# The gated sum of an encoder layer taken by halves of the tokens, its loads in order of use, and the w_out split moved from GpSimd to VectorE

## The chip, the core and the metric

One core of a Trainium2 chip runs the whole kernel. The metric is the device time of one execution in microseconds (us). The engines are TensorE (PE), VectorE (DVE), ScalarE (ACT), GpSimd (POOL) and SyncE (SP). Each works through its own list of instructions in order, and semaphores tie the lists together. Matmul results land in PSUM (8 banks of 128 x 512 fp32), everything else on the chip lies in SBUF, and DMAs bring data from HBM.

## What is computed

Two layers of an encoder over 1024 tokens and 1024 channels. The part that matters here, of one layer, is:

```
ya = mla_branch(...)                    # ends in  o @ w_oa,   o: 1024 x 512
merged = gates[:, :, 0] * ya + gates[:, :, 1] * yb + gates[:, :, 2] * yc
x = x + g1 * (merged @ w_out[l])
h2 = rmsnorm(x, norm2_g[l]) * (1.0 + sc2) + sh2
x = x + g2 * ec_moe(h2, w_router[l], w_gate[l], w_up[l], w_down[l])
```

`gates[0]` and the finished sum of the two other products are computed earlier and wait in HBM (`gate0d`, `partd`, 8 blocks of 128 channels x 1024 tokens each). `w_out` times `g1` also waits there (`woutd`). Products keep fp32 accuracy: an operand is split into `hi` (rounded by ACT) and `lo = x - hi` (a subtraction), and three matmuls (hi hi, hi lo, lo hi) replace one.

## The kernel before

The program is written in Python; a scheduler fixes the order of every engine's list when the kernel is built, and tiles of a pool are reused in rotation, so that a load waits until the last reader of its buffer is done.

After attention (lines 904 to 952) comes the **gated sum**: for each of the 8 blocks d of channels, `merge_mm` (L942) multiplies `w_oa` with `o` (`ohi`, `olo`: 4 blocks of 128 x 1024 tokens) into a PSUM tile of two banks, 24 matmuls of 512 columns, written by `mm3` (L319, the matmul at L325). `merge_gate` (L966) then takes each half of the tokens: loads `gate0d` (L970) and `partd` (L972) into two tiles `gh` (six buffers in all), multiplies (L973, one operand in PSUM), adds (L974, both in SBUF), and splits the result into the tiles `gm` by `split` (L114: a cast on ACT, a subtraction on VectorE, both at L115). The first two blocks stand around the last attention product `av(7, 3)`, whose result goes through `otmp` (L881) and `op` (L884) into `ohi` and `olo` of the second half of the tokens.

Meanwhile `w_out` is loaded in four quarters of 256 columns (`wout_load`, L980, 1 MB each) and split by `wout_split` (cast on ACT at L990, subtraction on POOL at L991).

Then comes the **output product**, one tile t of 128 tokens after the other (loop at L1227). `out_mm` (L1135, matmul at L1142) runs 96 matmuls of 256 columns for a tile; `residual` (L1145) adds the row of x, which ACT's list loads (L1229); `x_trans` (L1164) transposes the row on PE, `router` (L1177) multiplies it with the router, `soft` (L1185) makes a softmax. The tile t = 0 takes the quarters one by one and needs all 8 blocks d of the gated sum; from t = 1 on, the transposes, the router and, from t = 2 on, rounds of a top-k search on VectorE (`fills`, L1056) are woven in. The loads of the first expert weights (`prefetch`, L1033) start here too. SP issues all loads but the x rows.

The weights of `w_oa` lie in three pairs: `wo0` (columns 0 to 255), `wo1` (256 to 511) and `wo2` (512 to 1023, L996); their raw copies and those of `w_out` share two buffers named `raw`, and the pair of `wo2` takes buffers that `av(7, 3)` reads last.

Of the kernel before, what the change touches and what calls it, by code (L numbers as in the profile page):

```python
# [19 lines left out]
D = 1024  # L20
# [34 lines left out]
def encoder(ctx, tc, x, c, positions, w_mod, b_mod, norm1_g, w_in, b_gate, q_norm_g, w_uq, kv_norm_g,  # L55
# [271 lines left out]
    for l in range(DEPTH):  # L327
# [450 lines left out]
        with pool("att", side="right") as ap:  # L778
# [110 lines left out]

            LA = 2  # L890
# [13 lines left out]
            for n, (h, t) in enumerate(units):  # L904
# [6 lines left out]
                if n >= 1 and units[n - 1][1] % 2 == 1:  # L911
# [4 lines left out]
                    av(hh, g, *phl.pop((hh, g)), po[hh])  # L916
                if h % 2 == 0 and t == 2:
# [24 lines left out]
            def merge_mm(p, wo, c0, k0, k1):  # L942
                cs_ = slice(c0, c0 + 128)
                for k in range(k0, k1):
                    mm3(p, wo[0][:, k, cs_], wo[1][:, k, cs_], ohi[:, k], olo[:, k], k == 0, k == 3)
# [18 lines left out]
        wos = {}  # L964
# [12 lines left out]
        def wout_load(q):  # L977

            raw = W.tile([128, 8, 256], F32, name="raw", tag="raw")
            SP.dma_start(raw, woutd[l][:, :, 256 * q:256 * q + 256].rearrange("k p f -> p k f"))  # L980
            if q in (1, 2):
                hi, lo = (ring_tile([128, 8, 256]) for _ in range(2))
            else:
                hi = W.tile([128, 8, 256], F32R, name="whi", tag="whi")
                lo = W.tile([128, 8, 256], F32R, name="wlo", tag="wlo")
            wos[q] = (raw, hi, lo)

        def wout_split(q):
            raw, hi, lo = wos[q]
            ACT.copy(hi, raw)  # L990
            POOL.tensor_sub(lo, raw, f(hi))  # L991
            wos[q] = (hi, lo)
# [569 lines left out]
```

## Time and profile before

| | us |
|---|---|
| median of 3 runs | 3388.4 (3385.19 to 3395.47) |
| the profiled execution | 3388.24 |
| its span from the first to the last instruction | 3386.5 |
| PE busy | 3201.4 (95%) |
| VectorE busy | 2442.3 (72%) |
| ACT busy | 1857.7 (55%) |
| POOL busy | 384.2 (11%) |

The shares are means over stages. The stage between attention and the experts stands twice in the span, from about 900 and from about 2569 us, and the rows further down read the second. A row of a timeline gives start, length, engine, line, operation, output and inputs with their sizes, and in brackets how long the engine had been idle and what ended that.

### The profile page before, as it was taken

What the parts mean: (1) busy time and instruction counts of PE and PEld (TensorE: products, weight loads), DVE (VectorE), ACT (ScalarE), POOL (GpSimd) and SP (SyncE); (2) the same over time, 40 slices, a digit from 0 to 9 for tenths busy, and PEclk for the clock granted to TensorE, in tenths of its full rate; (3) what the DMA queues carried; (4) which work ended last, traced back from release to release, by engine and by line L of the source; (5) the groups of instructions that cost most, each with busy time, mean ns of one, the idle gap of its engine ahead of it and who ended that gap; (6) DMA issues with size and microseconds to landing.
All of it is one profiled execution on the core that took longest, in us unless ns stands there. A gap on an engine that the chain in (4) does not pass through costs nothing.

```text
span 3386.5 us, 43057 instructions
## 1 busy us (share of the span) xinstructions
PE 3201.4 (95%) x16593; PEld 2672.0 (79%) x16593; DVE 2442.3 (72%) x3730; ACT 1857.7 (55%) x2535; POOL 384.2 (11%) x364
## 2 busy tenths in 40 slices
PE   6999999999978899999989999999998969999996
PEld 5888887788877688888778888887887968888875
DVE  5556525599848899999864355338997489999997
ACT  5111213588634788887631121317885448888876
POOL 2001001000034001001020000010001330001010
PEclk8999999999988899999999999999999979999998
DMA  6346334000445899999622444340015559999994
GB/s 222 118 151 203 125 114 162 33 17 13 138 177 217 301 390 381 388 391 373 254 60 81 132 157 149 103 156 17 20 38 171 199 193 358 387 389 380 389 378 176
DMA packets 283374, 686.00 MB, mean 203 GB/s; under 512 B 24935, under 2 KB 139841, under 8 KB 283169
## 3 DMA queue, kind: packets, MB, share of 16 engines
q1 hardware_dynamic: 247008, 563.13, 44.8%
q0 software_dynamic: 33856, 111.74, 10.4%
q10 hardware_dynamic: 2304, 8.39, 0.7%
q8 instruction: 130, 2.13, 0.3%
q14 instruction: 76, 0.61, 0.1%
HBM read 607.63 MB, written 75.55 MB: 202 GB/s over the span
## 4 chain that ended last, share of the span: by engine, by line
PE 77%; DVE 12%; ACT 4%; DMA 3%; issue 2%; POOL 1%; SPq 0%; POOLq 0%; DVEq 0%; ACTq 0%
PE ps L325 62%; PE pa L1142 4%; DVE wlo L115 3%; PE pa L325 2%; DVE mx L846 2%; PE pa L864 2%; PE ps L1351 1%; PE pa L872 1%; PE pa L874 1%; DMA gh<-gate 1%; ACT pexp L851 1%; ACT whi L115 1%; DVE af L1065 1%; PE pa L1183 1%; DVE top L1063 1%
## 5 line engine op out<-in xcount | busy, mean ns | idle before, releaser
L115 DVE TENSOR_TENSOR wlo<-rg,whi 128x1024 fp32r<-128x1024 f32 x768 | 899.5, 1219 | 99.2 <-ACT whi L115 95.7
L115 ACT CAST whi<-rg 128x1024 fp32r<-128x1024 f32 x768 | 763.8, 1048 | 181.0 <-PE ps L325 181.0
L325 PE MATMUL ps<-whi,T 128*128 128x512 f32 x3072 | 841.8, 393 | 4.0 <-ACT T L115 2.2
L325 PEld LDWEIGHTS ps<-whi,T 128*128 128x128 f32 x3072 | 574.8, 189 | 126.4 <-ACT T L115 3.1
L325 PE MATMUL ps<-wlo,T 128*128 128x512 f32 x1536 | 489.1, 400 | 5.0 <-DVE wlo L115 3.0
L325 PE MATMUL ps<-hhi,whi 128*128 128x512 f32 x1376 | 427.4, 392 | 0.0
L325 PE MATMUL ps<-hlo,whi 128*128 128x512 f32 x1376 | 423.9, 389 | 0.0
L325 PE MATMUL ps<-hhi,wlo 128*128 128x512 f32 x1376 | 423.8, 389 | 0.0
L325 PEld LDWEIGHTS ps<-wlo,T 128*128 128x128 f32 x1536 | 281.3, 189 | 74.3 <-DVE wlo L115 19.0
L115 ACT CAST whi<-raw 128x2048 fp32r<-128x2048 f32 (+2 forms) x59 | 101.1, 1713 | 417.1 <-PE ps L325 360.8
L325 PEld LDWEIGHTS ps<-hhi,whi 128*128 128x128 f32 x1376 | 256.9, 188 | 58.9 <-issue 4.2
L325 PEld LDWEIGHTS ps<-hlo,whi 128*128 128x128 f32 x1376 | 258.3, 188 | 54.1
L325 PEld LDWEIGHTS ps<-hhi,wlo 128*128 128x128 f32 x1376 | 258.3, 188 | 54.0
L1142 PE MATMUL pa<-rg 128*128 128x256 f32 x768 | 191.4, 304 | 28.1 <-DVE rg L115 13.4
L115 DVE TENSOR_TENSOR wlo<-raw,whi 128x2048 fp32r<-128x2048 f32 (+2 forms) x59 | 120.9, 2050 | 98.5 <-ACT whi L115 98.5
L1142 PEld LDWEIGHTS pa<-rg 128*128 128x128 f32 x768 | 148.9, 206 | 31.3 <-DVE rg L115 14.5
L325 PE MATMUL ps<-khi,raw 128*128 128x512 f32 x512 | 166.5, 406 | 7.2 <-ACT pexp L851 5.7
L115 DVE TENSOR_TENSOR wlo<-pa,whi 128x512 fp32r<-128x512 f32 x256 | 169.3, 680 | 1.3 <-ACT whi L115 1.1
L1444 POOL DMA_INDIRECT xres<-y,idx x30 | 72.5, 2416 | 779.4 <-DVE y L1443 779.4
L851 ACT ACTIVATE pexp<-ps,nm 128x1024 f32<-128x1024 f32 x128 | 143.1, 1118 | 30.4 <-DVE nm L848 27.9
L846 DVE TENSOR_REDUCE mx<-ps 128x1 f32<-128x1024 f32 x128 | 155.0, 1212 | 5.4 <-PE ps L325 4.5
L115 ACT CAST whi<-pa 128x512 fp32r<-128x512 f32 x256 | 139.6, 588 | 7.6 <-PE pa L864 6.5
(409 smaller groups left out, 4899.6 us busy)
## 6 DMA issues: line engine op xcount, KB each, us to landing
rg<-in_w_gate_dram SPq DMA_DIRECT2D x128, 1024.0 KB, 8.9
rg<-in_w_up_dram SPq DMA_DIRECT2D x128, 1024.0 KB, 6.9
rg<-in_w_down_dram SPq DMA_DIRECT2D x128, 1024.0 KB, 7.8
raw<-in_w_mod_dram SPq DMA_DIRECT2D x48, 1024.0 KB, 5.4
raw<-in_w_in_dram SPq DMA_DIRECT2D x43, 1024.0 KB, 5.2
part<-pr POOLq DMA_DIRECT2D x32, 512.0 KB, 4.9
pr<-part POOLq DMA_DIRECT2D x16, 512.0 KB, 4.3
sq<-in_w_out_dram POOLq DMA_DIRECT2D x16, 512.0 KB, 4.4
```

The costliest lines, as they stand in the source:

```text
L115: return ACT.copy(hi, src), DVE.tensor_sub(lo, src, f(hi))
L325: PE.matmul(dst[:, s], a, b[:, s], start=start and i == 0, stop=stop and i == 2)
L846: DVE.reduce_max(mx, p, axis=AX.X)
L851: ACT.activation(e, p, AF.Exp, bias=nm, scale=SCALE, accum_out=sm)
L864: PE.transpose(p[:, 128 * k:128 * k + 128], e[:, o:o + 128], ident)
L872: PE.matmul(po[:, o:o + 256], vt[:, k, h, :], phi[:, k, :], start=(k == 0), stop=False, skip_group_check=True)
L874: PE.matmul(po[0:64, o:o + 256], vt[:, k, h, 0:64], plo[:, k, :], start=False, stop=(k == 7), skip_group_check=True)
L1063: DVE.max(v[:, 15 - r, :], a)
L1065: DVE.match_replace(a, v[:, 15 - r, :], a, -1.0)
L1142: PE.matmul(p[q // 2][:, 256 * (q % 2):256 * (q % 2) + 256], a, wos[q][b][:, k, :], skip_group_check=True, start=(k == 0 and i == 0 and q ...
L1183: PE.matmul(pls[t][:, :E], hT[:, 128 * k:128 * k + 128], wra[:, kk, :], start=(kk == 0), stop=(kk == 7))
L1444: POOL.indirect_dma_start(out=xres[l], in_=y, in_offset=None, compute_op=OP.add, out_offset=bass.IndirectOffsetOnAxis(ap=idx[e][:, 0:1], a ...
```

## The change

The gated sum runs by halves of the tokens: 16 units (hf, d) of 12 matmuls and one PSUM bank each, all d of the first half (tokens 0 to 511), then d = 2 to 7, 0, 1 of the second. The loads of a unit are issued three units ahead (`gate_load`), in the order in which the units use them. The load of `wo2` and the first three pairs of gate loads are written inside the attention loop. `w_out` is handled in four blocks (half of the columns, half of the rows) of 512 columns, loaded after units 3, 6, 9 and 11 and split after units 5, 8, 11 and 14, with the subtraction on VectorE (`split`). The output product uses 48 matmuls of 512 columns for a tile, and tile 0 takes the same form as the others. The rows of x for tiles 0 and 1 are loaded first, and the first four expert loads wait for the second of them.

```diff
+            merges = [(0, d) for d in range(8)] + [(1, (d + 2) % 8) for d in range(8)]
+            to_load, gates = list(merges), {}
+            def gate_load():
+                if to_load:
+                    hf, d = to_load.pop(0)
+                    s_ = slice(512 * hf, 512 * hf + 512)
+                    gates[hf, d] = [op_.tile([128, 512], F32, name="gh", tag="gg", bufs=6) for _ in range(2)]
+                    for t_, src in zip(gates[hf, d], (gate0d, partd)):
+                        SP.dma_start(t_, src[l][d][:, s_])
...
+                if h == H - 1 and t == 6:
+                    gate_load()
+                    wo1 = load_split(cols(w_oa[l], 256, 256), 4, 256)
+                    gate_load()
+                    wo2_raw = W.tile([128, 4, 512], F32, name="raw", tag="raw")
+                    SP.dma_start(wo2_raw, cols(w_oa[l], 512, 512))
+                    gate_load()
...
-            pm = [ps2(), ps2()]
-            merge_mm(pm[0], wo0, 0, 0, 3)
+            pm = [ps2() for _ in range(2)][1]
+            for d in range(2):
+                merge_mm(pm[:, 512 * d:512 * d + 512], wo0, 128 * d, 0)
             av(7, 3, *phl.pop((7, 3)), po[7])
-            merge_mm(pm[1], wo0, 128, 0, 3)
-            for d in range(2):
-                merge_mm(pm[d], wo0, 128 * d, 3, 4)
-        psum_open(3, 2)
+        psum_open(0, 8)
...
-        def merge_gate(p, d):
-            for hf in range(2):
-                s_ = slice(512 * hf, 512 * hf + 512)
-                g0 = op_.tile([128, 512], F32, name="gh", tag="gg", bufs=6)
-                SP.dma_start(g0, gate0d[l][d][:, s_])
-                pr = op_.tile([128, 512], F32, name="gh", tag="gg", bufs=6)
-                SP.dma_start(pr, partd[l][d][:, s_])
-                DVE.tensor_mul(g0, p[:, s_], g0)
-                DVE.tensor_add(g0, g0, pr)
-                split(gm[hf][0][d // 4][:, d % 4], gm[hf][1][d // 4][:, d % 4], g0)
+        def merge_gate(p, hf, d):
+            g0, pr = gates.pop((hf, d))
+            DVE.tensor_mul(g0, p, g0)
+            DVE.tensor_add(g0, g0, pr)
+            split(gm[hf][0][d // 4][:, d % 4], gm[hf][1][d // 4][:, d % 4], g0)
+            gate_load()
...
-            ACT.copy(hi, raw)
-            POOL.tensor_sub(lo, raw, f(hi))
...
+            split(hi, lo, raws.pop((c_, kh)))
...
+        wo2 = [W.tile([128, 4, 512], F32R, name=n_, tag=n_) for n_ in ("whi", "wlo")]
+        split(wo2[0], wo2[1], wo2_raw)
         for d in range(2):
-            merge_gate(pm[d], d)
-        for d in range(2, 8):
...
+            merge_gate(pm[:, 512 * d:512 * d + 512], 0, d)
+        for i, (hf, d) in enumerate(merges):
+            if i < 2:
+                continue
+            p = ps1()
+            wo, c0 = ((wo0, 0), (wo1, 256), (wo2, 512), (wo2, 512))[d // 2]
+            merge_mm(p, wo, 128 * d - c0, hf)
+            merge_gate(p, hf, d)
+            if i in (3, 6, 9, 11):
+                wout_load(*divmod((3, 6, 9, 11).index(i), 2))
+            if i in (5, 8, 11, 14):
+                wout_split(*divmod((5, 8, 11, 14).index(i), 2))
...
-                        for q in qs:
-                            PE.matmul(p[q // 2][:, 256 * (q % 2):256 * (q % 2) + 256], a, wos[q][b][:, k, :], skip_group_check=True,
-                                      start=(k == 0 and i == 0 and q == (fst[0] if q < 2 else 2)), stop=(k == 7 and i == 2))
+                    for i, (a, b) in enumerate(((a_hi, b_hi), (a_hi, b_lo), (a_lo, b_hi))):
+                        PE.matmul(p[c_], a, b, start=(k == 0 and i == 0), stop=(k == 7 and i == 2))
...
-            prefetch(2 + N_WM)
+            for t in range(2):
+                first = row_load_x(t)
+            prefetch(2 + N_WM, first)
```

How the order moves on SP, first layer, from the load of `wo2` (1 MB, `raw<-in_w_oa_dram`) on; `gh<-gate` and `gh<-part` are the two loads of a unit, `raw<-woutd` is a block of `w_out`. Before:

```order
L313 DMA raw_7395<-in_w_oa_dram 128x4x512
L970 DMA gh_7421<-gate00_85 128x512
L972 DMA gh_7423<-part0_83 128x512
L980 DMA raw_7401<-woutd0_88 128x8x256
L980 DMA raw_7480<-woutd0_88 128x8x256
L970 DMA gh_7429<-gate00_85 128x512
L972 DMA gh_7431<-part0_83 128x512
```

And now, to the fifth unit (number 4):

```order
L935 DMA raw_7302<-in_w_oa_dram 128x4x512
L901 DMA gh_7304<-gate00_85 128x512
L901 DMA gh_7305<-part0_83 128x512
L994 DMA raw_7447<-woutd0_88 128x4x512
L901 DMA gh_7393<-gate00_85 128x512
L901 DMA gh_7394<-part0_83 128x512
L994 DMA raw_7516<-woutd0_88 128x4x512
L901 DMA gh_7401<-gate00_85 128x512
L901 DMA gh_7402<-part0_83 128x512
```

The two first blocks of `w_out` no longer stand side by side, and the loads of one unit stand between them; the scheduler has put the block written after unit 6 ahead of unit 4's loads.

On VectorE, the middle of the gated sum. Before, one block d with both halves of the tokens (`gh<-ps` multiplies, `gh<-gh` adds, `rg<-gh` is the subtraction of the split):

```order
L973 TENSOR_TENSOR gh_7550<-ps_7525,gh_7550 128x512
L973 TENSOR_TENSOR gh_7558<-ps_7525,gh_7558 128x512
L974 TENSOR_TENSOR gh_7550<-gh_7550,gh_7552 128x512
L974 TENSOR_TENSOR gh_7558<-gh_7558,gh_7560 128x512
L115 TENSOR_TENSOR rg_7384<-gh_7550,rg_7382 128x512
L115 TENSOR_TENSOR rg_7388<-gh_7558,rg_7386 128x512
```

And now, the end of unit 8 and unit 9:

```order
L115 TENSOR_TENSOR rg_7383<-gh_7487,rg_7381 128x512
L986 TENSOR_TENSOR gh_7512<-pa_7564,gh_7512 128x512
L987 TENSOR_TENSOR gh_7512<-gh_7512,gh_7513 128x512
L115 TENSOR_TENSOR wlo_7632<-raw_7585,whi_7631 128x2048
L115 TENSOR_TENSOR rg_7561<-raw_7516,rg_7560 128x2048
L115 TENSOR_TENSOR rg_7383<-gh_7512,rg_7381 128x512
```

Two of the four subtractions of `w_out` (128x2048), which stood on POOL, stand side by side between the add and the subtraction of unit 9.

On PE, tile 0 of the output product at the first transpose. Before (`pa<-whi` and `pa<-wlo` are matmuls of the last quarter, `L1183` is the router):

```order
L1142 MATMUL pa_7731<-whi_7699,rg_7382 128x256
L1142 MATMUL pa_7731<-wlo_7700,rg_7382 128x256
L1142 MATMUL pa_7731<-whi_7699,rg_7384 128x256
L1169 MATMUL pa_7836<-ident_96,xo_7728 128x128 x4
L1183 MATMUL pa_7843<-wra_134,hT_7841 128x16 x4
```

And now:

```order
L1149 MATMUL pa_7769<-wlo_7632,rg_7377 128x512
L1149 MATMUL pa_7769<-whi_7631,rg_7379 128x512
L1175 MATMUL pa_7779<-ident_96,xo_7728 128x128 x4
L1149 MATMUL pa_7769<-whi_7631,rg_7377 128x512
L1149 MATMUL pa_7769<-wlo_7632,rg_7377 128x512
```

The transpose of tile 0's first half now stands after 33 of the tile's 48 matmuls instead of after all of its 96. VectorE's list still has the first residual of tile 0 behind the last subtraction of the gated sum, and ACT's list still has the loads of the x rows behind the last cast of it.

## Rows read from the trace of the kernel before

**Rows 1.** Chain of waits: start us, length us, what; last attention copy, first router, both layers

```profile
900.68 0.59 ACT otmp L881
...
975.01 1.06 PE pa L1183 x8
...
2569.24 0.59 ACT otmp L881
...
2643.60 1.06 PE pa L1183 x8
```

**Rows 2.** Stretches of the second layer: busy us and instructions by engine, clock, DMA

```profile
2569.30:2612.00 42.70, 40.63 (x171) 32.79 (x169) 28.70 (x34) 14.52 (x16) 13.45 (x3) 0.96 0.60 205
2612.00:2641.20 29.20, 15.29 (x96) 14.33 (x97) 15.75 (x18) 6.22 (x9) 6.75 (x4) 0.71 0.66 238
```

**Rows 3.** Timeline of PE, end of the gated sum and tile 0

```profile
2611.19 0.61 PE L325 MATMUL ps<-ohi,wlo 128*128 128x512 f32 x2
2613.13 2.39 PE L1142 MATMUL pa<-rg 128*128 128x256 f32 x18 [1.33 <-DVE gh L973]
...
2630.17 5.48 PE L1142 MATMUL pa<-rg 128*128 128x256 f32 x25 [4.07 <-DVE rg L115]
```

**Rows 4.** Timeline of VectorE, the whole gated sum of the second layer

```profile
2573.03 2.29 DVE L115 TENSOR_TENSOR wlo<-raw,whi 128x2048 fp32r<-128x2048 f32 x1 [1.11 <-ACT whi L115]
2575.24 1.28 DVE L973 TENSOR_TENSOR gh<-ps,gh 128x512 f32<-128x512 f32 x2
...
2582.48 0.69 DVE L973 TENSOR_TENSOR gh<-ps,gh 128x512 f32<-128x512 f32 x1 [2.36 <-DMA gh<-gate]
...
2595.68 0.69 DVE L973 TENSOR_TENSOR gh<-ps,gh 128x512 f32<-128x512 f32 x1 [4.48 <-DMA gh<-gate]
...
2597.66 5.53 DVE L115 TENSOR_TENSOR rg<-gh,rg 128x512 fp32r<-128x512 f32 x2
...
2612.30 0.69 DVE L973 TENSOR_TENSOR gh<-ps,gh 128x512 f32<-128x512 f32 x1 [4.73 <-DMA gh<-gate]
...
2619.54 0.69 DVE L973 TENSOR_TENSOR gh<-ps,gh 128x512 f32<-128x512 f32 x1 [2.65 <-DMA gh<-gate]
...
2623.93 5.59 DVE L974 TENSOR_TENSOR gh<-gh 128x512 f32<-128x512 f32 x2
2629.44 1.45 DVE L115 TENSOR_TENSOR rg<-gh,rg 128x512 fp32r<-128x512 f32 x2
```

**Rows 5.** Timeline of POOL, three of its four w_out subtractions

```profile
2597.08 4.96 POOL L991 TENSOR_TENSOR wlo<-raw,whi 128x2048 fp32r<-128x2048 f32 x1 [12.19 <-ACT whi L990]
2608.12 4.59 POOL L991 TENSOR_TENSOR rg<-raw,rg 128x2048 fp32r<-128x2048 f32 x1 [6.08 <-ACT rg L990]
2623.96 5.00 POOL L991 TENSOR_TENSOR wlo<-raw,whi 128x2048 fp32r<-128x2048 f32 x1 [11.25 <-ACT whi L990]
```

**Rows 6.** Chain of waits, runs of PE: 512 columns, 256 columns slow, 256 columns

```profile
2517.23 4.13 PE pa L325 x18
...
2644.66 3.28 PE pa L1142 x18
...
2648.80 2.97 PE pa L1142 x24
```

**Rows 7.** Tile gh over the whole span: issue to landing of its loads

```profile
DMA to landing us min/median/max: 2.6/3.8/7.8
```

**Rows 8.** Tile gh, loads issued from 2588 to 2591 us, behind a w_out load

```profile
DMA to landing us min/median/max: 6.9/6.9/7.0
```

**Rows 9.** Tile gh, loads issued from 2596 to 2599 us, with nothing ahead

```profile
DMA to landing us min/median/max: 2.8/2.8/2.8
```

**Rows 10.** Timeline of ACT: the loads of the x rows

```profile
2629.55 1.56 ACTq L1229 DMA_DIRECT2D xo<-xres  x3
```

**Rows 11.** Tile xo, the load issued from 2656 to 2658 us

```profile
DMA to landing us min/median/max: 3.2/3.2/3.2
```

**Rows 12.** Stretch of the sixth tile of the second layer, columns as in rows 2

```profile
2713.50:2728.00 14.50, 13.83 (x118) 13.66 (x117) 14.08 (x69) 6.84 (x13) 5.45 (x5) 1.00 0.29 110
```

More of the change, by code (lines that the diff above doesn't have):

```diff
@@ L1010, in encoder, with wout_load @@
-        wout_split(0)
-        wout_load(3)
-        wout_split(3)
+        wos, raws = {}, {}
+        def merge_gate(p, hf, d):
[4 more added lines that the diff above has]
+            gate_load()
+        def wout_load(c_, kh):
+            raws[c_, kh] = W.tile([128, 4, 512], F32, name="raw", tag="raw")
+            SP.dma_start(raws[c_, kh], woutd[l][4 * kh:4 * kh + 4, :, 512 * c_:512 * c_ + 512].rearrange("k p f -> p k f"))
@@ new lines, in wout_split @@
+        def wout_split(c_, kh):
+            if c_ == 0:
+                hi, lo = (ring_tile([128, 4, 512]) for _ in range(2))
+            else:
+                hi = W.tile([128, 4, 512], F32R, name="whi", tag="whi")
+                lo = W.tile([128, 4, 512], F32R, name="wlo", tag="wlo")
+            split(hi, lo, raws.pop((c_, kh)))
+            wos[c_, kh] = (hi, lo)
+        wo2 = [W.tile([128, 4, 512], F32R, name=n_, tag=n_) for n_ in ("whi", "wlo")]
+        split(wo2[0], wo2[1], wo2_raw)
@@ L1223, in aff_trans, with row_load_x @@
                     fill.extend([lambda r=r: top_round(i, r) for r in range(16)] + [lambda: merged(i)])
-            fst = [1]
-            prefetch(2 + N_WM)
+            def row_load_x(t):
+                xos[t] = op_.tile([128, D], F32, name="xo", tag="xo", bufs=3)
+                return ACT.dma_start(xos[t], x_in[128 * t:128 * t + 128, :])
+            for t in range(2):
+                first = row_load_x(t)
+            prefetch(2 + N_WM, first)
             for t in range(8):
-                xos[t] = op_.tile([128, D], F32, name="xo", tag="xo", bufs=3)
-                ACT.dma_start(xos[t], x_in[128 * t:128 * t + 128, :])
+                if t > 1:
+                    row_load_x(t)
                 p = [ps1()]
-                if t == 0:
-                    p.append(ps1())
-                    out_mm(t, p, (1,), 0, 8)
-                    out_mm(t, p, (2,), 0, 8)
-                    out_mm(t, p, (0,), 0, 8)
-                    residual(t, p, 0)
-                    out_mm(t, p, (3,), 0, 8)
-                    fst[0] = 0
-                    residual(t, p, 1)
-                    x_trans(t, 0)
-                    router(t, 0)
-                    continue
-                out_mm(t, p, (0, 1), 0, 3)
-                x_trans(t - 1, 1)
-                scale(t - 1)
-                out_mm(t, p, (0, 1), 3, 7)
-                router(t - 1, 1)
-                soft(t - 1)
-                h2_rows(t - 1)
-                if t == 7:
-                    with behind(softs[-1]):
-                        ACT.activation(small.tile([128, 1], F32, name="ms"), epsc, AF.Sqrt)
-                out_mm(t, p, (0, 1), 7, 8)
+                out_mm(t, p, 0, 0, 3)
+                if t > 0:
+                    x_trans(t - 1, 1)
+                    scale(t - 1)
+                out_mm(t, p, 0, 3, 7)
+                if t > 0:
+                    router(t - 1, 1)
+                    soft(t - 1)
+                    h2_rows(t - 1)
+                    if t == 7:
+                        with behind(softs[-1]):
+                            ACT.activation(small.tile([128, 1], F32, name="ms"), epsc, AF.Sqrt)
+                out_mm(t, p, 0, 7, 8)
                 residual(t, p, 0)
```

48 lines of the change are left out of this document (12 added, 36 removed).

## The prediction

> **What bounds the kernel now.** I read the chain of waits first. In each layer some 74.3 us pass from the last copy of attention to the router of tile 0: 975.01 - 900.68 in the first, 2643.60 - 2569.24 in the second [rows 1]. The two layers agree, so I work in the second and count twice. Next the stretches: in the gated sum PE is busy 40.6 of 42.7 us, but in the 29.2 us after it only 15.3, at a mean granted clock of 0.71 [rows 2]. So the gain to be had lies after the gated sum, not in it. PE's timeline tells why: the last matmul of the sum is done at 2611.8, tile 0 starts, and it can run through only from 2630.17, released by VectorE [rows 3]. Tile 0 needs all 8 blocks d, and the last subtraction of the last block ends at 2629.44 + 1.45 = 2630.9 [rows 4].
>
> So VectorE's list is the chain, and its 55.7 us from 2575.24 to 2630.9 [rows 4] can be taken apart. Work: 48 operations at 0.6 (two in a row take 1.28, of which 0.08 is the tail of the second [rows 4]) are 28.8. Waits for loads: 2.36 + 4.48 + 4.73 + 2.65 = 14.2 [rows 4]. Operations stretched beside POOL: 5.53 and 5.59 where two take 1.28 [rows 4], against POOL's 4.96 and 5.00 [rows 5], 4.3 each, 8.6 together. That makes 51.6; the rest is waits for casts and smaller stretches.
>
> What stretches is visible too: the multiply at 2612.30, with one operand in PSUM, took its 0.69 while POOL ran from 2608.12 to 2612.71 [rows 4, 5]; the adds and subtractions, with both in SBUF, did not. The Trainium skill (SBUF — State Buffer, "Who interferes with whom") says just this: a VectorE instruction with two SBUF inputs and a GpSimd instruction that reads SBUF exclude each other for the whole instruction. By that rule four POOL subtractions would put up to some 19 us on VectorE in a layer; the trace shows about 9, since VectorE was often waiting anyway, and the measurement decides.
>
> **The change part by part.** *Matmuls of the gated sum.* 192 as before, now each with weights of its own; 18 such took 4.13 [rows 6], 0.229 each. Two units (24 matmuls) stand ahead of the last attention product, in the order some three more than before, so it ends about 0.7 later, at 2569.7; the other 168 take 38.5: PE is done at 2608.2, against 2611.8. It needs no wait on the way: a unit reuses the bank of eight units before, and the second half's `ohi` is due only after eight units.
>
> *VectorE.* The cast of `wo2` waits for the last attention product and now stands before `otmp`: 2569.8 to 2571.7; its subtraction (2.29 [rows 4]) ends at 2574.0; then `op`, cast, `olo` and the two waiting subtractions of units 0 and 1, to 2577.3. From there:
> 14 units x 3 x 0.6 = 25.2;
> four `w_out` subtractions of 2.29 less the overlap, 2.25 each: 9.0, new on VectorE, with the 8.6 beside POOL gone in return;
> five places in the order where a subtraction stands right behind its own cast, 0.7 each: 3.5;
> waits for loads, which is the open term.
> A load lands in 2.8 us with nothing ahead [rows 9], in 6.9 behind a 1 MB block [rows 8], 2.6 to 7.8 over all [rows 7]. A unit's loads go out when the unit three before has given its buffers back. Following the order with 2.8, and 5.5 (between the two rows, nearer to the upper, since fewer small loads stand behind the blocks now) for a load right behind a block: unit 4's add waits about 1.3, unit 8's 2.3, unit 12's 2, unit 13 1.2, unit 15 1.7. Unit 8 as the example: unit 5 gives its buffers back at 2591.1, the gate goes out at 2591.2, the `w_out` block at 2591.8, the second load at 2592.4, which lands at 2597.9; VectorE stands at the add from 2595.6. Together about 9. Bounds: 0, and the 14.2 of today.
> The sum is 2577.3 + 25.2 + 9.0 + 3.5 + 9 = 2624.0; with the ends of the waits 2615 to 2629. Today it is 2630.9.
>
> *Tile 0.* Its first half of the columns needs only the first half's `gm` and `w_out` blocks split by about 2606, so PE goes on at 2608.2 and after 33 matmuls, at 2615.8, reaches the transpose. This needs the first residual, which stands behind the last subtraction on VectorE, and the row of x, whose load stands on ACT behind the last cast. Today that load is issued at 2629.55, at the end of the sum [rows 10], where 512 KB with nothing in the way land in 3.2 [rows 11]; the expert loads that stood beside it now wait for it. So: last cast 2624, row landed 2627.5, residual 0.7, transpose at 2628. PE idles 12 us. After such idling the clock is the lower of the two levels (1.2 GHz, not 2.4): 25 matmuls in 5.48, 0.22 each, against 24 in 2.97, 0.12 [rows 3, 6]. Hence transpose 0.7, 12 matmuls of 512 at 0.41 = 4.9, router 1.0, three matmuls 0.7: tile 1 starts at 2635.3. Today it starts at 2644.5, and its first 18 matmuls take 3.28 where 2.2 would do, with the transposes after them still slow [rows 6], about 1.6 lost, which I take as gone. Gain 9.2 + 1.6 = 10.8.
>
> *Tiles 1 to 7.* 96 x 0.12 = 11.5 becomes 48 x 0.229 = 11.0: 0.5 each while PE leads. In the sixth tile VectorE is busy 14.08 of 14.5 [rows 12], so there it is hidden. I count four tiles, 2.0 (bounds 0 and 3.7). The search after the last tile stays.
>
> *Loads of the gates and experts.* The experts' first four loads now start after the x rows, near 2628; first use is near 2787, so nothing waits. The rows `sh2` and `a2` on POOL come earlier, at 2608, 1 MB in the way of the last units' loads; that is in unit 13's 1.2.
>
> A layer gains 10.8 + 2.0 = 12.8, two layers 25.6. The profiled execution took 3388.24 (span 3386.5), the median is 3388.4: **3363**.
>
> **The rivals.** *VectorE keeps up*: no load waits, the sum ends at 2615, the transpose comes near 2619, a short idle; tile 1 at 2625. 19.5 + 1.6 + 3 = 24 a layer, 3340. For it: the loads are issued three units ahead in order of use. Against: the six buffers are the same, and the order puts two `w_out` blocks directly ahead of loads, one even between a unit's two.
>
> *The loads set the pace*: with 6.9 for each, three units take 6.9 + 2.8 (multiply, add, cast, subtract), 3.2 a unit, 45 for 14, and half of the 9.0 beside: the sum ends at 2627 to 2630. Tile 1 at 2641: 3.5 + 1.6 + 2 = 7 a layer, 3374. For it: 14.2 us of load waits today. Against: 2.8 where nothing stands ahead.
>
> *VectorE too loaded (slower).* The Trainium skill (Perfetto Trace Analysis, "Optimizing Scalar/DVE Operations") advises taking work off a saturated VectorE, and adds that between it and GpSimd this might not help, as they share a port; the change does the opposite of the advice. VectorE is busy 28.7 of 42.7 us in the sum, the stretched time included, so it is not saturated today [rows 2]. As a mechanism of this kernel: the four subtractions stand in VectorE's list, they free the `raw` buffers for which the next block's load waits, and SP's list holds the gate loads behind that. If every load lands only in the 7.8 of the slowest, three units take 10.6, 14 units 49.5, and with the 9.0 not hidden the sum ends at 2636, tile 1 starts at 2647. It turns into a loss when the sum ends later than 2637, that is with 22 us of load waits instead of 9; at 2640 the layer loses 3, the kernel 6: 3394.
>
> *The change does not do what it says*: if PE had to wait in the gated sum for its banks or for `wo2`, it would come out unchanged; the order gives `wo2` 3 us and the banks eight units of room. I give that no case of its own beyond "same".
>
> **How the numbers follow.** Chances: forecast (3350 to 3372) 0.57, VectorE keeps up (3328 to 3350) 0.18, loads set the pace (3372 to 3380) 0.17, slower than that up to no change (to 3398) 0.05, a loss 0.03. The forecast's own width is its load waits, 4 us a layer to either side, and 2 for the clock. A range of 3338 to 3377 leaves out about 0.07 below and 0.12 above. A measurement of this kernel can tell about 0.3%, 10 us, from no change: below 3378 is faster, 0.89; within 10, 0.08; above, 0.03.
>
> **What would show it right or wrong.** In the changed profile: the last matmul of the gated sum 39 us after the last attention copy; no stretched add or subtraction on VectorE; the last subtraction of the gated sum 55 us after that copy (46 for the first rival, 60 for the second); PE idle about 12 us before tile 0's transpose, with the x row as the releaser, and slow matmuls after it; tile 1 about 66 us after the copy, where it was 75; tiles of 13.8 us instead of 14.3. It is wrong above all if the load waits are not near 9 a layer, or if the x row or the residual is reached without waiting for the last unit.

## The result, and the profile after

| | before | after |
|---|---|---|
| median, us | 3386.8 | 3344.7 |
| ratio, 95% interval | | 0.9873, [0.9859, 0.9886] |
| span of the profiled execution, us | 3386.5 | 3342.1 |
| VectorE busy | 2442.3 (72%) | 2434.5 (73%) |
| POOL busy | 384.2 (11%) | 346.5 (10%) |

The change gains 42 us, where 25.6 were forecast. 3344.7 lies in the forecast range, beyond the forecast's own case and in that of the first rival. Neither case happened as it was described, though: a gain was underrated, the load waits that were forecast did not come, and a wait that the forecast had ruled out did. One of the four executions of the changed kernel took 9556 us, and one of the four with the split of `wo2` put back (further down) 5999 us; the ratios leave both out, and the medians of the other three are 3344.1 and 3347.0 us.

The zero point of all stages is the end of the last attention product, 2569.2 before (the copy L881 follows at once [rows 1]) and 2549.15 after (the cast of `wo2` follows at once). Chain of waits of the changed kernel, second layer (start, length, what); the last three rows are the first and the last router of the tiles and the first matmul of the experts:

```profile
2549.17 1.91 ACT whi L115
...
2554.16 40.52 PE pa L325 x167
...
2597.80 5.60 DMA xo<-xres
...
2607.66 0.80 PE pa L1189 x8
...
2713.03 1.90 PE pa L1189 x8
...
2745.07 1.04 PE ps L325 x2
```

And two rows of the chain of before that the forecast had not read, the same last router and first expert matmul:

```profile
2755.22 1.90 PE pa L1183 x8
2787.20 12.98 PE ps L325 x53
```

| us after the zero point | before | forecast | after |
|---|---|---|---|
| last matmul of the gated sum done | 42.6 | 39.0 | 45.5 |
| last subtraction of it done | 61.7 | 54.8 | 50.0 |
| tile 0's first transpose | | 58.8 | 55.1 |
| tile 1 starts | 75.4 | 66.1 | 60.0 |
| last tile's last router | 186.0 | 173.1 | 163.9 |
| first matmul of the experts | 218.0 | 205.2 | 195.9 |

(The forecast's last two rows: 66.1 and before's 110.6 for the tiles, less its 1.6 and 2.0; and 218.0 less its 12.8.) A layer gains 22.1 us here, 15.4 up to tile 1 and 6.7 in the tiles; two layers make the 44 of the spans. In the first layer the same stretch goes from 218.3 to 195.3.

Stretches of the second layer, columns as in rows 2:

```profile
2554.20:2560.00 5.80, 5.80 (x15) 4.60 (x16) 2.46 (x4) 1.60 (x3) 0.00 (x0) 0.57 0.74 271
2560.00:2594.70 34.70, 34.70 (x154) 28.72 (x153) 30.76 (x40) 13.97 (x15) 0.00 (x0) 1.00 0.69 220
2594.70:2604.20 9.50, 7.67 (x34) 6.01 (x32) 5.04 (x9) 1.85 (x3) 1.06 (x2) 1.00 0.74 285
```

PE's idle time has moved. Before, it stood behind the sum [rows 2]; now 4.9 us of it stand ahead of the sum's third unit (number 2), and the low clock behind it (0.57 of full speed) lets 15 matmuls take the time of 25. PE's timeline names both waits that are left:

```profile
2554.16 0.80 PE L325 MATMUL pa<-ohi,whi 128*128 128x512 f32 x1 [4.91 <-DVE op L884]
...
2604.24 0.66 PE L1175 MATMUL pa<-ident,xo 128*128 128x128 f32 x4 [1.87 <-DVE xo L1154]
```

VectorE's timeline, answering to rows 4:

```profile
2551.10 2.29 DVE L115 TENSOR_TENSOR wlo<-raw,whi 128x2048 fp32r<-128x2048 f32 x1 [1.19 <-ACT whi L115]
2553.43 0.68 DVE L884 TENSOR_TENSOR op<-pa,otmp 64x512 f32<-64x512 f32 x1
...
2559.53 0.69 DVE L986 TENSOR_TENSOR gh<-pa,gh 128x512 f32<-128x512 f32 x1 [2.65 <-PE pa L325]
...
2575.89 0.69 DVE L986 TENSOR_TENSOR gh<-pa,gh 128x512 f32<-128x512 f32 x1 [0.64 <-PE pa L325]
...
2597.84 1.30 DVE L115 TENSOR_TENSOR rg<-gh,rg 128x512 fp32r<-128x512 f32 x2
2603.49 0.69 DVE L1154 TENSOR_TENSOR xo<-xo,pa 128x512 f32<-128x512 f32 x1 [4.36 <-DMA xo<-xres]
```

No operation in the sum is stretched any more, and no row of this layer waits for a gate load. Over both layers the tile `gh` has this to say of its loads (what VectorE waited for, how often; then issue to landing, answering to rows 7):

```profile
  DMA gh<-gate: 0.2, 1
  DMA gh<-part: 0.2, 1
...
DMA to landing us min/median/max: 2.6/3.1/5.3
```

So VectorE's chain, from unit 2's multiply (2559.53) to the last subtraction (2599.1), is 39.6 us of work and short waits for casts and PE, with no load in it.

### The profile page after: what moved, and what is told of

It reads as the page before. It is cut to its first block, busy times and chain, and to the rows that moved or that the text cites. A ratio compares the mean times of both kernels' runs of the same rounds, so it can differ in the third digit from the quotient of the medians.

```text
span 3342.1 us, 41527 instructions
## 1 busy us (share of the span) xinstructions
PE 3178.8 (95%) x15825; PEld 2616.3 (78%) x15825; DVE 2434.5 (73%) x3738; ACT 1857.3 (56%) x2535; POOL 346.5 (10%) x356
## 3 DMA queue, kind: packets, MB, share of 16 engines
q1 hardware_dynamic: 242912, 563.13, 45.5%
## 4 chain that ended last, share of the span: by engine, by line
PE 79%; DVE 12%; ACT 4%; issue 2%; DMA 2%; POOL 1%; SPq 0%; POOLq 0%; DVEq 0%; ACTq 0%
PE ps L325 63%; PE pa L325 4%; PE pa L1149 4%; DVE wlo L115 4%; DVE mx L846 2%; PE pa L864 2%; PE ps L1353 1%; PE pa L872 1%; PE pa L874 1%; ACT whi L115 1%; ACT pexp L851 1%; PE pa L1189 1%; DVE af L1072 1%; DVE pexp L854 1%; DVE T L115 0%
## 5 line engine op out<-in xcount | busy, mean ns | idle before, releaser
L115 ACT CAST whi<-raw 128x2048 fp32r<-128x2048 f32 (+2 forms) x63 | 108.7, 1726 | 428.0 <-PE ps L325 370.5
L325 PEld LDWEIGHTS ps<-hhi,whi 128*128 128x128 f32 x1376 | 256.9, 188 | 58.8 <-issue 4.2
L115 DVE TENSOR_TENSOR wlo<-raw,whi 128x2048 fp32r<-128x2048 f32 (+2 forms) x63 | 130.1, 2065 | 99.9 <-ACT whi L115 99.8
L229 DVE SCALAR_TENSOR_TENSOR macc<-raw,csil,macc 128x256 f32<-128x256 f32 x280 | 135.0, 484 | 8.4
L864 PE MATMUL pa<-ident,pexp 128*128 128x128 f32 x1024 | 135.2, 273 | 2.6 <-DVE nm L848 1.8
```

The lines of the kernel that those rows point to most:

```text
L115: return ACT.copy(hi, src), DVE.tensor_sub(lo, src, f(hi))
L229: DVE.scalar_tensor_tensor(acc, raw[:, k], csil[:, k:k + 1], acc, op0=OP.mult, op1=OP.add)
L325: PE.matmul(dst[:, s], a, b[:, s], start=start and i == 0, stop=stop and i == 2)
L864: PE.transpose(p[:, 128 * k:128 * k + 128], e[:, o:o + 128], ident)
```

## Experiments

Of each run the median and the ratio to the kernel before, run beside it on the same chip, are given; the changed kernel itself stands at 0.9873. One thousandth of the ratio is 3.4 us. Single medians of the kernel before went from 3386 to 3389 in these runs, so ratios are compared, not times.

### One part alone, and one part undone: the w_out subtractions

In the kernel before:

```diff
-            POOL.tensor_sub(lo, raw, f(hi))
+            DVE.tensor_sub(lo, raw, f(hi))
```

> The kernel before, with one part of the change alone: the four w_out subtractions on VectorE instead of POOL, nothing else moved. Theory A (8.6 us of stretch a layer goes, 9.0 of work comes, both on the chain): no change, 3384 to 3390 against 3387. Theory B (the 9.0 fall into the 14.2 us of load waits, the 8.6 are gone): up to 8.6 us a layer, 3370 to 3376. Theory C (the stretch is as long as all of POOL's subtractions, 19 us a layer): 3365 or less.

Measured: 3367.1 us, ratio 0.9936 [0.9920, 0.9953]: 21 us faster, with this one word. That lies between theory B (3370 to 3376) and theory C (3365 or less); theory A is out. The waits of VectorE for gate loads in the second layer (what `gh` waited for, us and times) were 14.2 [rows 4]; they are now

```profile
  DMA gh<-gate: 4.9, 4
  DMA gh<-part: 2.8, 2
```

7.7 together: 6.5 less, against 9.0 us of new work, and the stretch is gone. The loads themselves landed no faster (median 5.1 us in this layer, 4.9 before), so I read the 6.5 as work standing where VectorE had stood still; no run separates that from loads that were issued earlier. The chain from the last copy to the first router, 74.4 us before [rows 1], is 64.6:

```profile
2558.75 0.59 ACT otmp L881
...
2623.32 1.49 PE pa L1183 x8
```

Of the 9.8 us, 6.6 are the earlier end of the sum (55.1 us after that copy instead of 61.7), and 3.2 come in tile 0.

And the other way round, in the changed kernel:

```diff
-            split(hi, lo, raws.pop((c_, kh)))
+            raw = raws.pop((c_, kh))
+            ACT.copy(hi, raw)
+            POOL.tensor_sub(lo, raw, f(hi))
```

> The changed kernel with the four w_out subtractions back on POOL. Theory A (each POOL subtraction holds VectorE's instructions with two SBUF operands up for its length, 4.3 us seen in the trace of before): VectorE loses 4 x 2.25 of work and gains up to 4 x 4.3 of stretch, so the sum ends up to 8 us later a layer: 3353 to 3361 us, with adds and subtractions of some 5 us. Theory B (the stretch is small where VectorE's work is spread evenly): VectorE ends up to 9 us earlier, but PE's last unit ends at 2594.7 all the same, so at most 2 us a layer come of it: 3341 to 3346.

Measured: 3370.4 us, 0.9948 [0.9931, 0.9964]: 25 us slower than the changed kernel, more than theory A's upper end. POOL's four subtractions in the timeline, and the four rows of VectorE beside them:

```profile
2581.15 4.63 POOL L1004 TENSOR_TENSOR rg<-raw,rg 128x2048 fp32r<-128x2048 f32 x1 [77.67 <-ACT rg L1003]
2595.61 4.64 POOL L1004 TENSOR_TENSOR rg<-raw,rg 128x2048 fp32r<-128x2048 f32 x1 [9.84 <-DMA gh<-gate]
2600.21 5.05 POOL L1004 TENSOR_TENSOR wlo<-raw,whi 128x2048 fp32r<-128x2048 f32 x1
2612.99 4.55 POOL L1004 TENSOR_TENSOR wlo<-raw,whi 128x2048 fp32r<-128x2048 f32 x1 [7.73 <-ACT whi L1003]
```

```profile
2582.00 4.33 DVE L115 TENSOR_TENSOR rg<-gh,rg 128x512 fp32r<-128x512 f32 x1 [0.69 <-ACT rg L115]
...
2596.41 4.39 DVE L987 TENSOR_TENSOR gh<-gh 128x512 f32<-128x512 f32 x1
2600.72 5.69 DVE L115 TENSOR_TENSOR rg<-gh,rg 128x512 fp32r<-128x512 f32 x2
...
2613.83 4.25 DVE L115 TENSOR_TENSOR rg<-gh,rg 128x512 fp32r<-128x512 f32 x1 [0.69 <-ACT rg L115]
```

Each of the four holds a VectorE operation up until POOL is done: 18.7 us for what takes 3.4 (0.69 for one, 1.29 for two), 15.3 of stretch, against 18.9 of POOL's work. In the trace of before the forecast saw 8.6, beside two of the four. Beside the two others VectorE was standing at a load for part of POOL's time: for 2.36 and 4.73 us [rows 4], with POOL at work from 2580.28 to 2584.89 and from 2608.12. Only one more add, at 2583.21, was stretched there, to 2.23. Most of the rest is waits for casts: 12 of 0.69 in this layer where the changed kernel has 4. The sum ends 62.4 us after the product instead of 50.0, and 15.3 - 9.0 + 8 x 0.69 = 11.8 of the 12.4 are these.

The Trainium skill (SBUF — State Buffer, "Who interferes with whom") says that the two instructions exclude each other. These rows agree, and where VectorE's list is full its price, up to 18.9 here, is nearer to the 15.3 measured than the 8.6 that the forecast took from the trace of before.

### PE's wait in the gated sum

Unit 2 is the first matmul group with a bank of its own after the last attention product, and that bank is the one the product was written to. Its reader `op` (L884) stands on VectorE behind the subtraction of `wo2`. Two runs take the wait away. Another bank for unit 2, one bank being reserved for the last unit:

```diff
-        psum_open(0, 8)
+        psum_open(0, 7)
+        low = pstate["pool"].tile([128, 512], F32, name="pl", tag="pl", bufs=1)
...
-            p = ps1()
+            p = low if i == 15 else ps1()
```

> The changed kernel, but unit 2 of the gated sum gets a PSUM bank other than the one of the last attention product. Theory A: PE's 4.91 us wait before unit 2 is for that bank alone (its reader op, L884, stands behind the split of wo2), and the slow clock after it (0.57) costs some 2 us more; the loads have room. Without it PE runs on at 2549.1. VectorE, free from 2556.9, then needs 14 x 3 x 0.6 + 9.0 + 3.5 = 37.7 and ends the gated sum near 2595 instead of 2599.1; the x row hangs on the last cast, so tile 0's transpose comes 4 us earlier a layer: 3337 us (3335 to 3341), with PE idle for some 5 us before the transpose instead of 1.9. Theory B: the load waits of the forecast (9 a layer) are only away because this wait gave the loads 7 us more; they come back and eat the gain: 3343 to 3346, with several us of VectorE waiting for DMA. Theory C: PE waits for something else (wo2): unchanged, 3345.

Measured: 3349.7 us, 0.9888 [0.9871, 0.9904], no gain. PE did run from the product (its end is 2550.20 here) to the end of the sum at 2588.3 without a wait, 38.1 us, near the forecast's 38.5. But VectorE ended at 2599.4, 49.2 us after the product instead of 50.0, and three of its rows wait for loads:

```profile
2575.47 0.69 DVE L988 TENSOR_TENSOR gh<-gh 128x512 f32<-128x512 f32 x1 [0.68 <-DMA gh<-part]
...
2595.08 0.69 DVE L987 TENSOR_TENSOR gh<-pl,gh 128x512 f32<-128x512 f32 x1 [1.79 <-DMA gh<-gate]
...
2597.37 0.69 DVE L988 TENSOR_TENSOR gh<-gh 128x512 f32<-128x512 f32 x1 [0.40 <-DMA gh<-part]
```

2.9 us in place of the 3.3 (2.65 and 0.64) that VectorE had waited for PE: theory B by its mechanism. The edit also has a fault. The bank it reserved goes to tile 0 next, and tile 0 now stands until unit 15's multiply has read it; after this wait its matmuls are slow (8.15 us for 24, where the changed kernel takes 5.60):

```profile
2595.91 8.15 PE L1150 MATMUL pa<-rg 128*128 128x512 f32 x24 [7.59 <-DVE gh L987]
```

The other way is to put the split of `wo2` back where it was before the change:

```diff
-        split(wo2[0], wo2[1], wo2_raw)
+        with behind(*last_o[-1]):
+            split(wo2[0], wo2[1], wo2_raw)
```

> The changed kernel, but the split of wo2 stands behind the cast and subtraction of the last attention product (ohi, olo), as it did before the change; the bank stays. Theory A (the wait for op): op is done 1.4 us after the last attention product instead of 5, so PE waits 1.4 us; wo2 is ready some 6.5 us after the product, unit 4 is due 6.9 after it. PE ends the gated sum some 5 us earlier, VectorE some 3 to 4: 3338 us (3336 to 3342). Theory B (load waits come back): 3343 to 3346. Theory C (PE needs wo2 that early): unit 4 now waits instead of unit 2, 3345 or more.

Measured: 3348.8 us, 0.9884 [0.9864, 0.9904], no gain either. PE's wait fell to 1.43 us, yet VectorE waits 7.7 us for loads in this layer and ends 51.3 after the product:

```profile
2562.53 0.69 DVE L986 TENSOR_TENSOR gh<-pa,gh 128x512 f32<-128x512 f32 x1 [1.69 <-DMA gh<-gate]
2564.53 0.69 DVE L986 TENSOR_TENSOR gh<-pa,gh 128x512 f32<-128x512 f32 x1 [0.57 <-DMA gh<-gate]
2575.93 0.69 DVE L987 TENSOR_TENSOR gh<-gh 128x512 f32<-128x512 f32 x1 [2.14 <-DMA gh<-part]
2587.93 0.69 DVE L987 TENSOR_TENSOR gh<-gh 128x512 f32<-128x512 f32 x1 [0.64 <-DMA gh<-part]
2597.10 0.69 DVE L986 TENSOR_TENSOR gh<-pa,gh 128x512 f32<-128x512 f32 x1 [2.67 <-DMA gh<-gate]
```

PE then waits 6.73 us for the residual ahead of tile 0's transpose, and is slow behind it. The second `w_out` block waits for the raw buffer of `wo2`, which now comes free some 2 us later, and SP holds the gate loads behind it; I take this for the reason that the loads are later than in the run with the bank, but no run separates it.

### The x row of tile 0

The row landed in 5.6 us and not in the 3.2 of rows 11. Loading the rows of tiles 0 and 1 early, into a buffer that a `w_out` block gives back near 2585:

```diff
+            rows01 = W.tile([128, 2, D], F32, name="raw", tag="raw")
...
-                xos[t] = op_.tile([128, D], F32, name="xo", tag="xo", bufs=3)
+                xos[t] = rows01[:, t] if t < 2 else op_.tile([128, D], F32, name="xo", tag="xo", bufs=3)
```

> The changed kernel, but the x rows of tiles 0 and 1 are loaded into a buffer of w_out blocks that comes free near 2585 (second layer), instead of one that the gated sum's matmuls read to their end. Theory A: only the row's landing (5.6 us) stands between the last cast and tile 0's transpose; with the row there, the transpose follows 33 matmuls after the sum's end, near 2602.4 instead of 2604.24: 1.9 us a layer, 3341 us (3340 to 3343). Theory B: 1 MB more among the loads of the gates brings load waits of 1 to 3 us a layer: 3343 to 3348.

Measured: 3355.6 us, 0.9908 [0.9892, 0.9925], 12 us slower than the changed kernel, worse than theory B. The two rows, issued at 2588.57, and the first expert loads behind them, at 2599.83, are now among the last gate loads:

```profile
2595.11 0.69 DVE L987 TENSOR_TENSOR gh<-gh 128x512 f32<-128x512 f32 x1 [2.97 <-DMA gh<-part]
...
2609.66 0.69 DVE L987 TENSOR_TENSOR gh<-gh 128x512 f32<-128x512 f32 x1 [4.87 <-DMA gh<-part]
```

> Both edits together: another bank for unit 2, and the x rows loaded early. Theory A: PE ends the sum near 2588.3, VectorE near 2595, the transpose after 33 matmuls comes near 2596.3 instead of 2604.24: 7.9 us a layer, 3329 us (3327 to 3334); PE has no idle stretch over 1 us between the last attention product and tile 1, and the clock stays at 1.00. Theory B (the loads set the pace once PE does not wait): 3336 to 3343, with VectorE waiting for DMA in the sum.

Both edits together: 3351.0 us, 0.9890 [0.9874, 0.9907]. That is above both theories. VectorE waits 5.0 us for loads in the layer, and tile 0 stands 10.28 us for the reserved bank, the fault of the bank edit again.

What stood in the row's way was something else, the rows `sh2` and `a2`, the two loads that POOL's list issues here the moment PE's sum ends (2594.96 and 2595.49), ahead of the row at 2597.80. POOL's timeline in the changed kernel:

```profile
2594.96 0.54 POOL L254 DMA_DIRECT2D sh<-modrow  x1 [103.44 <-PE pa L325]
2595.49 0.54 POOL L254 DMA_DIRECT2D a<-gain  x1
```

```diff
-            bcast_row(sh2, mod_bcast(l, 3))
-            bcast_row(a2, gain_bcast(1, l))
...
-            for t in range(2):
-                first = row_load_x(t)
+            first = row_load_x(0)
+            for dst, src in ((sh2, mod_bcast(l, 3)), (a2, gain_bcast(1, l))):
+                gated(POOL.dma_start(dst, src), first)
+            first = row_load_x(1)
```

> The changed kernel, but the rows sh2 and a2 (2 x 512 KB on POOL's queue), which it issues the moment the gated sum's last matmul is done, now wait for the x row of tile 0. Theory A: they are why that row lands in 5.6 us and not in the 3.2 of before; with them behind it the row lands in about 3.2, the residual comes at 2601, and the transpose is bound by PE's 33 matmuls, near 2602.3 instead of 2604.24: 1.9 us a layer, 3341 us. Theory B: the row is slow because of the last gate loads and of the two other x rows issued with it: it still takes 5 us or more, 3344 to 3346.

Measured: 3342.9 us, 0.9867 [0.9850, 0.9883]. The size is that of theory A, but the interval cannot tell it from the changed kernel. The mechanism is in the trace: VectorE stands 2.08 us for the row where it was 4.36, and PE goes from the sum through 33 matmuls into the transpose without a wait. Two runs that did not touch these rows agree: where they went out well ahead of the x row of tile 0, it landed in 3.2 us (10 us ahead, with the split of `wo2` put back) and 3.3 (4.7 ahead, with the subtractions on POOL).

```profile
2600.76 0.69 DVE L1152 TENSOR_TENSOR xo<-xo,pa 128x512 f32<-128x512 f32 x1 [2.08 <-DMA xo<-xres]
```

### The size of the matmuls, and the halves

```diff
-                        PE.matmul(p[c_], a, b, start=(k == 0 and i == 0), stop=(k == 7 and i == 2))
+                        for q in range(2):
+                            PE.matmul(p[c_][:, 256 * q:256 * q + 256], a, b[:, 256 * q:256 * q + 256], skip_group_check=True,
+                                      start=(k == 0 and i == 0 and q == 0), stop=(k == 7 and i == 2))
```

> The changed kernel with the output product in matmuls of 256 columns, 96 a tile, each left operand used for both halves, as before the change. Theory A (the size of the matmuls is worth what the tiles gained in the middle, 0.25 to 0.37 us each): 8 tiles x 0.3 = 2.5 us a layer, 3350 us. Theory B (it is worth all that the tile phase gained, 6.8 us a layer): 3358 us, with the slow clock of before in the last tile. Theory C (VectorE hides it): 3345.

Measured: 3355.5 us, 0.9903 [0.9887, 0.9920], 10 us slower than the changed kernel, 5 a layer, between theories A and B. Its routers (chain of waits; tiles 0, 1, 7):

```profile
2613.80 0.80 PE pa L1191 x8
...
2628.06 0.80 PE pa L1191 x8
...
2724.13 1.90 PE pa L1191 x8
```

A tile takes 14.26 us where the changed kernel takes 13.88 (2607.66 to 2621.54), and all of them 110.3 where it takes 105.4. Up to the second router of the seventh tile that makes 2.1; the other 2.9 come behind it. There PE's two longest waits are for VectorE, 0.79 and 1.25 us in the changed kernel:

```profile
2706.13 0.19 PE L1104 MATMUL pa<-negid,aff 128*32 128x32 f32 x1 [0.79 <-DVE aff L1201]
...
2711.52 0.66 PE L1175 MATMUL pa<-ident,xo 128*128 128x128 f32 x4 [1.25 <-DVE xo L1154]
```

and 1.69 and 2.67 us with 256 columns, 2.3 more:

```profile
2715.34 0.19 PE L1104 MATMUL pa<-negid,aff 128*32 128x32 f32 x1 [1.69 <-DVE aff L1203]
...
2722.23 1.12 PE L1177 MATMUL pa<-ident,xo 128*128 128x128 f32 x4 [2.67 <-DVE xo L1156]
```

Why VectorE is later there, no run shows. The clock is not the same in the two kernels with 256 columns. In that of before it had fallen to 0.50, the lower of its two levels (1.2 GHz, not 2.4), behind a first wait of 1.70; in this run it stayed at 1.00 behind 1.69 and fell only behind 2.67. The wait of before, and the stretch behind it; then a stretch of this run that holds the wait of 1.69:

```profile
2746.26 0.19 PE L1097 MATMUL pa<-negid,aff 128*32 128x32 f32 x1 [1.70 <-DVE aff L1195]
```

```profile
2749.00:2752.00 3.00, 3.00 (x16) 3.00 (x16) 2.70 (x17) 0.00 (x0) 0.41 (x1) 0.50 1.03 375
```

```profile
2714.00:2718.00 4.00, 2.66 (x29) 2.65 (x29) 3.90 (x7) 1.48 (x6) 3.62 (x3) 1.00 1.03 420
```

Taking the units of the sum by blocks again:

```diff
-            merges = [(0, d) for d in range(8)] + [(1, (d + 2) % 8) for d in range(8)]
+            merges = [(0, 0), (0, 1), (1, 0), (1, 1)] + [(hf, d) for d in range(2, 8) for hf in range(2)]
```

> The changed kernel with the units of the gated sum by blocks d, both halves of the tokens of one d in a row, instead of all d of the first half first. Theory A (the halves only make tile 0 independent of the last units): unit 2 now needs the last attention product's own split, 1.4 us more of waiting for PE; tile 0's first matmuls need unit 14, whose split ends 3 us after PE's last matmul of the sum. 1 to 3 us a layer: 3347 to 3351 us. Theory B (the halves are what keeps VectorE from standing still): 3355 or more. Theory C: no part of the gain, 3345.

Measured: 3344.3 us, 0.9882 [0.9865, 0.9898]. It cannot be told from the changed kernel: 3 us slower by the middles of the ratios, and 2 faster by the profiled spans (3340.0 here). Theory C and the lower end of theory A fit; theory B does not. PE's wait is the same 4.92 us for `op`: unit 2 uses the last product only in its last three matmuls, and by then its split is done. The gate loads still went out three units ahead, in the order of use; no run undid that.

### Several edits together

Unit 2 with another bank, the reserved one going to unit 9, and `sh2` and `a2` behind the x row (as above):

```diff
-            p = ps1()
+            p = low if i == 9 else ps1()
```

> The changed kernel with two edits: unit 2 gets another PSUM bank (this time unit 9, not the last unit, takes the bank of the last attention product, so tile 0 does not wait for it), and sh2 and a2 wait for the x row of tile 0. Theory A: PE ends the sum 38 us after the last attention product and does not wait at tile 0's first matmul; VectorE ends some 47 to 49 us after it, the row lands 3.4 us after the last cast, the transpose comes near 51 instead of 55.1, and the clock falls in the 4 to 5 us that PE idles before it: 3337 us (3334 to 3341). Theory B: without PE's wait VectorE waits for loads for as long as PE had waited: 3341 to 3344, no better than with sh2 and a2 alone.

Measured: 3336.9 us, 0.9861 [0.9844, 0.9877], theory A's size, though the interval overlaps those of the changed kernel and of the run with `sh2` and `a2` alone. PE waits 4.40 us for the residual, whose row VectorE had awaited for 2.31, and then runs slow:

```profile
2594.75 1.12 PE L1174 MATMUL pa<-ident,xo 128*128 128x128 f32 x4 [4.40 <-DVE xo L1153]
```

With the x row of tile 0 alone loaded early, `sh2`, `a2` and the expert loads behind that of tile 1, and the last `w_out` subtraction behind the first residual:

```diff
-                xos[t] = op_.tile([128, D], F32, name="xo", tag="xo", bufs=3)
+                xos[t] = W.tile([128, D], F32, name="raw", tag="raw") if t == 0 else op_.tile([128, D], F32, name="xo", tag="xo", bufs=3)
...
             for t in range(2):
                 first = row_load_x(t)
+            for dst, src in ((sh2, mod_bcast(l, 3)), (a2, gain_bcast(1, l))):
+                gated(POOL.dma_start(dst, src), first)
             prefetch(2 + N_WM, first)
...
-                residual(t, p, 0)
+                added = residual(t, p, 0)
+                if t == 0:
+                    wout_split(1, 1, added)
```

> Four edits on the changed kernel: unit 2 with another bank; the x row of tile 0 alone loaded early, into a w_out buffer; sh2, a2 and the first expert loads behind the x row of tile 1; the last w_out subtraction behind the first residual. Theory A: PE ends the sum 38 us after the last attention product, VectorE near 46 to 47, the transpose follows at 47.7 instead of 55.1, with under 2 us of idle PE: 7 us a layer, 3330 us (3327 to 3336). Theory B: the row, 512 KB among the last gate loads, makes the last units wait as two rows and the expert loads did (up to 7.8 us): 3338 to 3345.

Measured: 3335.8 us, 0.9852 [0.9836, 0.9868], at theory A's upper end. The residual came 47.1 us after the product, as expected; PE waited 2.09 for it, and 0.62 more for the moved subtraction (`wlo`, 2598.12 to 2600.4). Then the last of these edits was taken out again, against the version before:

```diff
-                added = residual(t, p, 0)
-                if t == 0:
-                    wout_split(1, 1, added)
+                residual(t, p, 0)
```

> The kernel of the four edits less one: unit 2 with another bank, the x row of tile 0 alone loaded early, sh2, a2 and the expert loads behind the x row of tile 1; the last w_out subtraction is back at its place in the changed kernel. Theory A: what is left in the two-edit kernel is the row (the residual stood 2.3 us for it, PE 4.0, then the slow clock); with the row there the residual follows the last subtraction, near 49 us after the last attention product instead of 50: 1 to 2 us a layer less, 3333 us (3330 to 3336). Theory B: the row among the last gate loads costs VectorE what it saves: 3336 to 3340.

Measured: 3335.3 us, 0.9846 [0.9828, 0.9864], span 3333.5, in theory A's range. It is the lowest median, some 9 us under the changed kernel by the middles of the ratios (the two intervals still share 0.9859 to 0.9864); the three last versions cannot be told from each other. Nor do the traces say that the moved subtraction cost anything: in the second layer the experts start 189.5 us after the product with it and 192.6 without, in the first 195.1 and 191.3. PE runs through the sum at full clock, and its one wait stands ahead of the transpose:

```profile
2593.29 1.11 PE L1174 MATMUL pa<-ident,raw 128*128 128x128 f32 x4 [3.70 <-DVE raw L1153]
```

with slow matmuls after it (1.11 for four transposes, 0.66 in the changed kernel). Up to this transpose VectorE's list is the bound, and loads are 2.3 us of its waits.

## Why the prediction was right, and where it was not

The sign, the place (the chain from attention to tile 1) and the range held. The gain was forecast at 25.6 us and came to 42, so the time fell in the range only because that was wide enough to hold the first rival; and by the forecast's own test ("wrong above all if the load waits are not near 9 a layer") its central term failed. The parts, each undone alone in the changed kernel: 25 for the subtractions on VectorE, 10 for the 512 columns, 3 or nothing for the halves. Parts undone one by one need not add up to the whole; what is left, a few us, may lie with the order of the loads and the x rows, which no run undid.

*The subtractions on VectorE* were counted as 9.0 of new work against 8.6 of stretch, a draw. They are the largest part of the gain. Two terms were mis-sized: the stretch that goes is 15.3 a layer where VectorE's list is full, and against the 9.0 of work that comes the load waits fell by 6.5 when nothing else was moved. The 14.2 us of load waits that the forecast had read [rows 4] were the room for it.

*The load waits*, 9 a layer in the sum, were near nothing (0.4 in both layers together). Part of the reason is a wait that the forecast had excluded: with PE's wait gone and `wo2` early, the situation that it had worked out, they are 2.9; with `wo2` late, 7.7. Even the 2.9 is a third of the forecast. There the unit that it took as its example, unit 8, waited 0.68 where it had 2.3, units 4, 12 and 13 not at all where it had 4.5, and unit 15 2.2 where it had 1.7. In the changed kernel the longest landing was 5.3, where the forecast had 5.5 for every load right behind a block. With PE feeding one unit after another, a load issued three units ahead has 8 us less the time in which its buffer is given back; that this spacing is why the term was too large is argued, not shown.

*"It needs no wait on the way: a unit reuses the bank of eight units before"* failed for the first unit, which has no unit eight before it. Its bank is that of the last attention product, and the forecast's own list had `op` behind the subtraction of `wo2`. It cost 4.9 us and a slow clock, so PE's sum ended at 45.5 and not 39.0. On the whole path it cost little: VectorE lost 3.3 and had no load waits, and taking the wait away alone gained nothing. Together with a free bank for tile 0 and edits to the x row the ratios are 4 to 9 us lower by their middles, but no interval separates the part of this wait. That one error hid behind the other, a wait for PE in place of waits for loads, was luck.

*The end of the sum on VectorE*: 50.0 instead of 54.8. 9 of load waits less, 2.65 more for the wait for unit 2 and 0.64 for PE later make 49.1. The rest is a balance of small terms: the 42 operations from unit 2 on take 0.65 each and not 0.6 (an add stands 0.72 behind its own multiply), 2.0 more, and casts, `w_out` subtractions and an earlier start 1.1 less.

*Tile 0*: the x row as the releaser was right, its size was not (5.6 against 3.2). The forecast had put `sh2` and `a2` in the way of the last units' loads; they stood in the way of this row. PE idled 1.9 there and not 12: it came out of the sum 6.5 later, as its idling had come earlier, and the transpose came 3.7 sooner, as VectorE's sum ended sooner. Tile 0 ran at full clock: 4.9 us from the transpose to tile 1 instead of 7.3. Tile 1 came at 60.0, 6.1 ahead of the forecast.

*Tiles 1 to 7*: the pace was right, 13.9 us instead of 14.25, the patch of slow clock behind tile 0 nearly too (1.6 forecast; from the first router to the second it was 8.0 us before and 7.1 with 256 columns, 0.9). What was missed is the last tile: 512 columns are worth 5.0 a layer, above the upper bound of 3.7, as the forecast had read one tile in the middle [rows 12] and not the last one, where PE's two waits for VectorE are 2.3 us shorter with 512 columns.

*The rivals.* "VectorE keeps up" gave the time (3340), with its mechanism half right: no load waits, but the sum's end at 50 and not at 46. "Loads set the pace" shows only in part, once PE's wait is taken away: load waits of 2.9 and 7.7 us, with the sum's end at 49.2 and 51.3 and not at 60. "VectorE too loaded" points the wrong way: the work that it feared is the largest part of the gain.

## What to carry to other kernels

An engine that waits for loads has room in its list: price work moved onto it against those waits first (here 9.0 us of work, and 6.5 less of waiting). Price two engines that hold each other up by the length of the other engine's work (18.9 here, of which 15.3 came), not by the stretch seen while the first one stood at loads (8.6). When a pool is opened anew, look up for its first tile which instruction last reads the bank, and what stands ahead of that instruction. A transfer that decides a stage needs the queues of all engines looked at for what starts in the same microseconds.

## What the runs showed that had not been expected

A subtraction of 128x2048 takes 2.28 us on VectorE and 4.55 to 5.05 on POOL, and a VectorE operation with both operands in SBUF that starts in it ends only after POOL's is over (4.33 for 0.69).

A wait of PE can cost more than its length, but its length alone does not say whether. Slow matmuls followed waits of 2.67, 3.70, 4.40, 4.91 and 6.73 us in these rows, and the clock stayed at 1.00 behind waits of 0.79, 1.69, 1.87 and 2.09; yet it fell behind 1.70 in the last tile of before (0.50 from 2749 to 2752) and behind 1.25 in that of the changed kernel (0.79 from 2711 to 2714). What made the difference there is open.

One wait taken away turned up three times on other engines: as load waits (2.9 and 7.7 us), as a wait for a bank (7.59), and as PE's wait for the first residual (4.40).
